# Local attention: two heads at once in the score products, native float32 in the value products

## Chip, cores and metric

The kernel runs on one core of a Trainium2 chip. The metric is the device time of one execution in microseconds; the kernel before takes 2477.17 us (median of 3 runs, 2470.8 to 2479.98).

## What is computed

A trunk of two layers on 512 tokens of width 1024. In each layer three mixers read the same normalised input `h`: (A) latent attention, (B) a gated recurrence in both directions, (C) attention in a window of 128 tokens to either side. Their outputs go through a projection each, are weighted by a gate and added; cross attention and a feed-forward block follow. The change lies in mixer C:

```python
q = q.reshape(Bsz, nb, C_BLOCK, C_KV_HEADS, G, C_DH)      # 8 heads of 64, 2 key heads, blocks of 128
s = einsum('bnqkgd,bnskd->bnkgqs', q, kb) * C_DH ** -0.5 + bias      # span of 3 blocks of keys
s = where(valid, s, MASK_VALUE)
m = maximum(max(s, axis=-1), sink_l)
p = exp(s - m)
p = p / (sum(p, axis=-1) + exp(sink_l - m))
o = einsum('bnkgqs,bnskd->bnqkgd', p, vb)
```

Everything is float32, and the result is compared with a float32 reference.

## The kernel before

Activations lie with the model dimension on the 128 partitions and the 512 tokens along the row. A product in near-float32 precision is made of three products in the one-pass type `fp32r`: every operand is split into a rounded part and a remainder (`split`, L177: a copy on ScalarE and a subtraction on VectorE), and `mm3` (L153) adds high·high, high·low and low·high in PSUM. Weights come from HBM as a stream of units of four 128x128 blocks in the order in which they are used (`_fetch`, L110, on SyncE's DMA queue; `_part`, L116, splits them); five buffers of raw and of split units let the stream run ahead. A projection of 1024 rows into 128 columns (`projs`, L164) is 24 matmuls of 512 columns and takes two units.

PSUM has eight banks, all of one pool (`bank`, L105). SBUF holds 25 buffers of 2 KB a partition (`t2`) and 14 of 8 KB (`c8`). A planner puts the instructions on each engine's queue: it goes by the order in the program as long as an instruction's inputs and its buffer are there, takes a later one where they are not, and places the semaphore waits. Every engine then works its queue strictly in that order.

Mixer C is `window_pre` (L698: keys, values and the first query, each a projection) and `window` (L726). One 128-row tile of the query holds two heads of 64 rows: head `bq` in rows 0 to 63 and head `bq + 4` in rows 64 to 127; the key tile has the two key heads in the same way. `window` goes through the eight heads one after the other, `i = 2 * bq + e`:

- `scores(bq, e)`, L742: fetches the head's bias block by DMA (L746), multiplies for each of four query blocks 64 rows of the query with 64 rows of keys (three products, 256 keys wide for the first and last block, 384 for the others), adds the bias out of PSUM into SBUF (L756), takes the row maximum (L757), and makes the normalised weights: maximum with the sink (L759), exponentials on ScalarE with their sums (L760, L762), sum, reciprocal, four multiplications (L764 to L767).
- the turn, L781 to L789: ten 128x128 transposes by TensorE, four banks, each split into a high and a low part.
- `values()`, L795: for four key blocks three products of the value block (128 columns, both key heads) with the turned weights. Only the 64 output rows of the head's own key head are kept (L802).

The scores of head `i + 1` are made behind the turn of head `i` and ahead of its values. Between a head's scores and its turn stand *fillers*: projections of mixer A's branch (`branch`, L507), put into a list and taken from it by `fill` (L186): two gates for an even head, for an odd head one `out` (two projections of four row blocks each, as long as one gate) and the projection of the next query (L780), whose split (`query`, L735) comes behind the turn. Mixer A (`mla`, L590) has the same stages; its values (`values`, L659) are native float32 products of 64 columns, two heads in the two column halves of the array.

Of the kernel before, what the change touches and what calls it, by code (L numbers as in the profile page):

```python
# [10 lines left out]
F32R = mybir.dt.float32r  # L11
I32 = mybir.dt.int32
AF = mybir.ActivationFunctionType
ALU = mybir.AluOpType
AX = mybir.AxisListType

P = 128
D = 1024
T = 512
# [19 lines left out]
V_GMIX, V_GX, V_GMEM, V_GFFN, V_GQ, V_GKV, V_GOUT, V_SINK, V_N = 0, 8, 16, 24, 32, 35, 37, 38, 46  # L39
# [36 lines left out]
class _K:  # L76
# [621 lines left out]
    def window_pre(self, l, h):  # L698

        st = self.wst_ = {}  # L700

        def step(nm, cols):
            def run():
                b, = self.projs("w_in", l, np.arange(D), [cols], h)
                if nm == "k":
                    kv = st["kv"] = self.c8([P, 4, T], F32R)
                    self.split(kv[:, 0], kv[:, 1], b)
                elif nm == "q":
                    st["q"] = (self.t2(F32R), self.t2(F32R))
                    self.split(st["q"][0], st["q"][1], b, scale=0.125)  # L710
                else:
                    kv = st["kv"]
                    vf = self.t2()
                    self.nc.scalar.activation(vf, b, AF.Copy)
                    tb = self.bank([P, 4, P])
                    for j in range(4):
                        self.nc.tensor.transpose(tb[:, j], vf[:, j * P:(j + 1) * P], self.ident)
                    st["v"] = [kv[:, 2 + i].rearrange("p (a b) -> p a b", a=4) for i in range(2)]
                    self.split(st["v"][0], st["v"][1], tb)
            return run  # L720
        return [step("k", O_KC + np.arange(P)), step("v", O_VC + np.arange(P)), step("q", self.qcol(0))]

# [3 lines left out]
    def window(self, l, h, y, before):  # L726
        nc = self.nc
        lv = V_N * l
        allr = np.arange(D)
        kv = self.wst_["kv"]  # L730
        k = (kv[:, 0], kv[:, 1])
        qt = self.wst_["q"]
        vh, vl = self.wst_["v"]

        def query(b):  # L735
            qt = (self.t2(F32R), self.t2(F32R))
            self.split(qt[0], qt[1], b, scale=0.125)
            return qt

        spans = [(P if j == 0 else 0, 256 if j == 3 else 384) for j in range(4)]  # L740

        def scores(bq, e):  # L742
            hd = bq + 4 * e
            a = slice(64 * e, 64 * e + 64)
            bias = self.t2(shape=(P, 384))
            nc.sync.dma_start(bias, self.biasd[hd])  # L746
            s = [self.t2(shape=(P, 384)) for _ in range(4)]
            st = self.sm(16, "smw", 4)
            nm, sm, es, rs = st[:, 0:4], st[:, 4:8], st[:, 8:12], st[:, 12:16]
            for j, (lo, hi) in enumerate(spans):  # L750
                sb = self.bank()
                js = slice(j * P, (j + 1) * P)
                ks = slice((j - 1) * P + lo, (j - 1) * P + hi)
                o = sb[:, :hi - lo]
                self.mm3(o, (qt[0][a, js], qt[1][a, js]), (k[0][a, ks], k[1][a, ks]), True, True)
                nc.vector.tensor_tensor(s[j][:, lo:hi], o, bias[:, lo:hi], op=ALU.add)  # L756
                nc.vector.reduce_max(nm[:, j:j + 1], s[j][:, lo:hi], axis=AX.X)  # L757
            sink = self.col(lv + V_SINK + hd)
            nc.vector.tensor_scalar(nm, nm, sink, -1.0, op0=ALU.max, op1=ALU.mult)  # L759
            nc.scalar.activation(es, nm, AF.Exp, bias=sink)  # L760
            for j, (lo, hi) in enumerate(spans):
                nc.scalar.activation(s[j][:, lo:hi], s[j][:, lo:hi], AF.Exp, bias=nm[:, j:j + 1],  # L762
                                     accum_out=sm[:, j:j + 1])
            nc.vector.tensor_tensor(es, es, sm, op=ALU.add)  # L764
            nc.vector.reciprocal(rs, es)
            for j, (lo, hi) in enumerate(spans):
                nc.vector.tensor_scalar(s[j][:, lo:hi], s[j][:, lo:hi], rs[:, j:j + 1], None, op0=ALU.mult)  # L767
            return s

        s = scores(0, 0)  # L770
        before()
        for i in range(8):
            bq, e = i // 2, i % 2
            a = slice(64 * e, 64 * e + 64)
            if i % 2 == 0:
                self.fill(2)
            else:
                self.fill(1 if bq < 3 else 2)
                if bq < 3:
                    qb = self.projs("w_in", l, allr, [self.qcol(bq + 1)], h)[0]  # L780
            pta, ptb = self.c8([P, 4, 384], F32R), self.c8([P, 4, 384], F32R)  # L781
            for kb in range(4):
                qs = [j for j in (kb - 1, kb, kb + 1) if 0 <= j < 4]
                tb = self.bank()
                for n, j in enumerate(qs):
                    c = (kb - j + 1) * P
                    nc.tensor.transpose(tb[:, n * P:(n + 1) * P], s[j][:, c:c + P], self.ident)  # L787
                w = len(qs) * P
                self.split(pta[:, kb, :w], ptb[:, kb, :w], tb[:, :w])  # L789
            if i < 7:  # L790
                if e == 1:
                    qt = query(qb)
                s = scores((i + 1) // 2, (i + 1) % 2)

            def values():  # L795
                o = self.bank()
                for kb in (0, 3, 1, 2):
                    q0 = max(kb - 1, 0) * P
                    w = 256 if kb in (0, 3) else 384
                    x = (pta[:, kb, :w], ptb[:, kb, :w])  # L800
                    self.mm3(o[:, q0:q0 + w], (vh[:, kb], vl[:, kb]), x, kb == 0, kb == 2)
                self.split(y[bq][0][a], y[bq][1][a], o[a])  # L802
            if i < 7:
                values()
        return values

    def memstat(self):

# [337 lines left out]
```

## Time and profile before

| | |
|---|---|
| median of 3 runs | 2477.17 us (2470.8 to 2479.98) |
| profiled execution | 2471.43 us, of which the span from first to last instruction is 2469.6 us |
| TensorE matmul busy | 2422.0 us, 98% |
| TensorE weight loads | 1999.7 us, 81% |
| VectorE / ScalarE / GpSimd busy | 1545.8 / 1215.4 / 262.6 us |
| granted clock of TensorE, mean | 0.995 |

Matmuls are pipelined, so that the busy times of neighbours overlap; the time from one start to the next says more than the length of one. Helpers hide the place of an instruction: nearly all products are of line 151, and they are told apart by the tiles and shapes. `128*64` is a product of 128 rows and 64 columns of the array; `64*128` one of 64 rows.

### The profile page before, as it was taken

What the parts mean: (1) busy time and instruction counts of PE and PEld (TensorE: products, weight loads), DVE (VectorE), ACT (ScalarE), POOL (GpSimd) and SP (SyncE); (2) the same over time, 40 slices, a digit from 0 to 9 for tenths busy, and PEclk for the clock granted to TensorE, in tenths of its full rate; (3) what the DMA queues carried; (4) which work ended last, traced back from release to release, by engine and by line L of the source; (5) the groups of instructions that cost most, each with busy time, mean ns of one, the idle gap of its engine ahead of it and who ended that gap; (6) DMA issues with size and microseconds to landing.
All of it is one profiled execution on the core that took longest, in us unless ns stands there. A gap on an engine that the chain in (4) does not pass through costs nothing.

```text
span 2469.6 us, 32711 instructions
## 1 busy us (share of the span) xinstructions
PE 2422.0 (98%) x12038; PEld 1999.7 (81%) x12038; DVE 1545.8 (63%) x2787; ACT 1215.4 (49%) x2213; POOL 262.6 (11%) x197
## 2 busy tenths in 40 slices
PE   8999999999999999999998999999999999999998
PEld 6788877788888888888877887887888888888886
DVE  8888666676665655355577776766766656553553
ACT  7666565455554533233466665654554445332332
POOL 2455300000000000000035542000000000000000
PEclk9999999999999999999999999999999999999999
DMA  4211322223453333333421222221224523333332
GB/s 140 70 61 55 90 74 60 63 73 100 140 138 98 86 95 98 96 96 98 129 73 60 69 74 63 73 64 60 81 79 149 146 78 89 97 96 98 98 96 76
DMA packets 119681, 220.96 MB, mean 89 GB/s; under 512 B 13281, under 2 KB 15585, under 8 KB 119137
## 3 DMA queue, kind: packets, MB, share of 16 engines
q1 hardware_dynamic: 119520, 218.88, 30.1%
q8 instruction: 94, 1.54, 0.3%
q14 instruction: 67, 0.54, 0.1%
HBM read 214.63 MB, written 4.19 MB: 89 GB/s over the span
## 4 chain that ended last, share of the span: by engine, by line
PE 82%; DVE 8%; issue 4%; ACT 3%; POOL 2%; DMA 1%; SPq 0%; DVEq 0%; ACTq 0%; POOLq 0%
PE ps L151 80%; POOL t L404 2%; DVE c L457 1%; PE ps L643 1%; DVE smx L411 1%; ACT whi L120 1%; POOL t L408 1%; DVE c L439 1%; DVE t L411 1%; DVE wlo L121 1%; PE ps L787 0%; DVE c L438 0%; DVE zz L482 0%; DMA c<-in_memT_dram 0%; DVE t L434 0%
## 5 line engine op out<-in xcount | busy, mean ns | idle before, releaser
L151 PE MATMUL ps<-c,whi 128*128 128x512 f32 (+1 forms) x5696 | 1734.7, 386 | 6.2 <-ACT whi L120 6.0
L151 PEld LDWEIGHTS ps<-c,whi 128*128 128x128 f32 x5696 | 1061.0, 188 | 227.7 <-issue 10.8
L151 PE MATMUL ps<-c,wlo 128*128 128x512 f32 (+1 forms) x2848 | 1098.9, 386 | 15.3 <-DVE wlo L121 15.2
L120 ACT ACTIVATE whi<-wraw 128x512 fp32r<-128x512 f32 x764 | 475.2, 630 | 841.7 <-PE ps L151 621.6
L121 DVE TENSOR_TENSOR wlo<-wraw,whi 128x512 fp32r<-128x512 f32 x764 | 520.2, 690 | 533.9 <-ACT whi L120 516.6
L151 PEld LDWEIGHTS ps<-c,wlo 128*128 128x128 f32 x2848 | 536.4, 188 | 126.7 <-DVE wlo L121 20.2
L151 PE MATMUL ps<-c,t 128*128 128x512 f32 (+4 forms) x896 | 185.6, 386 | 4.3 <-DVE c L181 2.8
L404 POOL TENSOR_SCALAR t<-t 128x512 f32<-128x512 f32 x32 | 71.7, 2242 | 1081.2 <-ACT t L401 1079.7
L151 PEld LDWEIGHTS ps<-c,t 128*128 128x128 f32 (+2 forms) x896 | 133.9, 182 | 43.6 <-issue 16.9
L457 POOL TENSOR_TENSOR c<-c,smx 128x256 f32<-128x256 f32 x128 | 145.0, 1161 | 74.3 <-DVE c L438 64.3
L966 DVE TENSOR_TENSOR t<-ps,t 128x512 f32<-128x512 f32 x112 | 76.2, 688 | 103.1 <-PE ps L151 103.1
L180 ACT ACTIVATE c<-ps 128x512 fp32r<-128x512 f32 (+3 forms) x200 | 97.7, 527 | 84.1 <-PE ps L151 81.3
L181 DVE TENSOR_TENSOR c<-ps,c 128x512 fp32r<-128x512 f32 (+3 forms) x200 | 114.9, 598 | 28.5 <-ACT c L180 27.4
L151 PE MATMUL ps<-c 128*32 128x32 f32 (+3 forms) x1280 | 108.1, 255 | 5.5 <-DVE c L439 5.5
L151 PEld LDWEIGHTS ps<-c 128*32 128x32 f32 (+2 forms) x1280 | 94.9, 148 | 21.3 <-DVE c L439 4.0
L948 DVE TENSOR_TENSOR c<-ps,c 128x512 f32<-128x512 f32 x64 | 44.2, 690 | 73.0 <-PE ps L151 73.0
L457 DVE TENSOR_TENSOR c<-c,smx 128x256 f32<-128x256 f32 x128 | 67.7, 587 | 0.3
L181 DVE TENSOR_TENSOR c<-t,c 128x512 fp32r<-128x512 f32 (+1 forms) x84 | 51.9, 633 | 2.9 <-ACT c L180 2.9
L408 POOL TENSOR_TENSOR t<-t,t 128x512 f32<-128x512 f32 x32 | 44.7, 1397 | 84.1 <-ACT t L407 84.1
L180 ACT ACTIVATE c<-t 128x512 fp32r<-128x512 f32 (+1 forms) x84 | 47.8, 581 | 9.4 <-DVE t L390 3.3
L406 ACT ACTIVATE t<-t 128x512 f32<-128x512 f32 x32 | 20.1, 629 | 62.4 <-POOL t L404 62.4
L411 DVE TENSOR_TENSOR_SCAN t<-cst,t 128x512 f32<-128x512 f32 x32 | 40.8, 1275 | 15.8 <-POOL t L408 15.8
(144 smaller groups left out, 1888.7 us busy)
## 6 DMA issues: line engine op xcount, KB each, us to landing
wraw<-in_w_dram SPq DMA_DIRECT2D x764, 256.0 KB, 2.7
c<-in_xT_dram SPq DMA_DIRECT2D x16, 256.0 KB, 5.1
t<-in_bias_dram SPq DMA_DIRECT2D x16, 192.0 KB, 2.8
c<-in_memT_dram SPq DMA_DIRECT2D x3, 1024.0 KB, 8.0
xs<-c SPq DMA_DIRECT2D x8, 256.0 KB, 2.4
c<-xs SPq DMA_DIRECT2D x8, 256.0 KB, 4.3
out_dram<-t SPq DMA_DIRECT2D x8, 256.0 KB, 2.0
t<-in_rope_dram SPq DMA_DIRECT2D x4, 256.0 KB, 3.1
```

The costliest lines, as they stand in the source:

```text
L120: self.nc.scalar.activation(hi, raw, AF.Copy)
L121: self.nc.vector.tensor_tensor(lo, raw, hi.bitcast(F32), op=ALU.subtract)
L151: self.nc.tensor.matmul(o, a, b, start=start, stop=stop)
L180: nc.scalar.activation(hi, src, AF.Copy)
L181: nc.vector.tensor_tensor(lo, src, hi.bitcast(F32), op=ALU.subtract)
L404: nc.gpsimd.tensor_scalar(g, f, TINY, KNEE, op0=ALU.max, op1=ALU.min)
L408: nc.gpsimd.tensor_tensor(f, f, g, op=ALU.add)
L411: scan = lambda o, m, x: nc.vector.tensor_tensor_scan(o, m, x, 0.0, op0=ALU.mult, op1=ALU.add)
L439: nc.vector.scalar_tensor_tensor(ki, kk, omlb, cc, op0=ALU.mult, op1=ALU.mult)
L457: eng.tensor_tensor(ov, sv, ev, op=ALU.mult)
L948: nc.vector.tensor_tensor(x[c], b, xold[c], op=ALU.add)
L966: self.nc.vector.tensor_tensor(t, b, r, op=ALU.mult)
```

## The change

The scores of two heads are made together, their products alternating between the array's row halves, in two banks for each block; adding the bias and taking the maximum is one instruction, which starts from the sink. The turned weights are copied once in float32 instead of being split, and the values are one native float32 product a head and block, 64 columns wide, both heads into one bank. The query's projection comes ahead of the odd head's filler.

```diff
-        def scores(bq, e):
-            hd = bq + 4 * e
...
+        def scores(bq):
+            hds = [bq, bq + 4]
+            biases, ss, sts, os = [], [], [], []
+            for e in range(2):
+                bias = self.t2(shape=(P, 384))
+                nc.sync.dma_start(bias, self.biasd[hds[e]])
...
             for j, (lo, hi) in enumerate(spans):
-                self.mm3(o, (qt[0][a, js], qt[1][a, js]), (k[0][a, ks], k[1][a, ks]), True, True)
-                nc.vector.tensor_tensor(s[j][:, lo:hi], o, bias[:, lo:hi], op=ALU.add)
-                nc.vector.reduce_max(nm[:, j:j + 1], s[j][:, lo:hi], axis=AX.X)
+                os.append([self.bank()[:, :hi - lo] for _ in range(2)])
+                for n, (qi, ki) in enumerate(((0, 0), (0, 1), (1, 0))):
+                    for e in range(2):
+                        a = slice(64 * e, 64 * e + 64)
+                        self.mm(os[j][e], qt[qi][a, js], k[ki][a, ks], n == 0, n == 2)
+                for e in range(2):
+                    nc.vector.tensor_tensor_reduce(ss[e][j][:, lo:hi], os[j][e], biases[e][:, lo:hi], 1.0,
+                                                   self.col(lv + V_SINK + hds[e]), ALU.add, ALU.max,
+                                                   sts[e][0][:, j:j + 1])
...
+        def turned(s):
+            pt = self.c8([P, 4, 384])
...
-                self.split(pta[:, kb, :w], ptb[:, kb, :w], tb[:, :w])
+                if kb % 2 == 0:
+                    nc.scalar.activation(pt[:, kb, :w], tb[:, :w], AF.Copy)
+                else:
+                    nc.vector.tensor_copy(pt[:, kb, :w], tb[:, :w])
...
-                    self.mm3(o[:, q0:q0 + w], (vh[:, kb], vl[:, kb]), x, kb == 0, kb == 2)
-                self.split(y[bq][0][a], y[bq][1][a], o[a])
+                    for e in range(2):
+                        a = slice(64 * e, 64 * e + 64)
+                        self.mm(o[a, q0:q0 + w], v[:, kb, a], pts[e][:, kb, :w], kb == 0, kb == 2)
+                self.split(y[bq][0], y[bq][1], o)
...
+        ss = scores(0)
+        before()
+        for bq in range(4):
+            self.fill(2)
+            pts = [turned(ss[0])]
+            if bq < 3:
+                qb = self.projs("w_in", l, allr, [self.qcol(bq + 1)], h)[0]
+                self.fill()
+            else:
+                self.fill(2)
+            pts.append(turned(ss[1]))
+            pend = values(bq, pts)
+            if bq < 3:
+                qt = query(qb)
+                ss = scores(bq + 1)
+                pend()
+        return pend
```

## Rows read from the trace of the kernel before

**Rows 1.** The page: span, and busy time, share and instructions of each engine.
```profile
span 2469.6 us, 32711 instructions
PE 2422.0 (98%) x12038; PEld 1999.7 (81%) x12038; DVE 1545.8 (63%) x2787; ACT 1215.4 (49%) x2213; POOL 262.6 (11%) x197
```
**Rows 2.** The page: the chain that ended last, shares of the span by engine.
```profile
PE 82%; DVE 8%; issue 4%; ACT 3%; POOL 2%; DMA 1%; SPq 0%; DVEq 0%; ACTq 0%; POOLq 0%
```
**Rows 3.** Windows of the stage in either layer: busy time (count) by engine, clock, DMA.
```profile
476.46:613.70 137.24, 136.63 (x698) 115.02 (x697) 93.87 (x217) 74.66 (x172) 0.00 (x0) 1.00 0.28 84
1765.20:1842.00 76.80, 76.39 (x395) 65.42 (x394) 50.80 (x116) 41.68 (x94) 0.00 (x0) 1.00 0.27 83
```
**Rows 4.** TensorE in order of time, odd head: start, us, what, count.
```profile
493.03 1.25 PE L787 MATMUL ps<-cst,t 128*128 128x128 f32 x10
494.21 2.04 PE L151 MATMUL ps<-c,t 64*128 64x256 f32 x12
496.18 2.02 PE L151 MATMUL ps<-c,c 128*128 128x256 f32 x12
498.05 0.63 PE L151 MATMUL ps<-c,whi 128*128 128x512 f32 x2
```
**Rows 5.** TensorE in order of time, the even head after it.
```profile
508.97 1.25 PE L787 MATMUL ps<-cst,t 128*128 128x128 f32 x10
510.43 2.02 PE L151 MATMUL ps<-c,t 64*128 64x256 f32 x12 [0.21 <-ACT t L183]
512.38 0.74 PE L151 MATMUL ps<-c,c 128*128 128x256 f32 x4
```
**Rows 6.** Groups by shape, whole span: half of the score matmuls.
```profile
L151 PE MATMUL ps<-c,t 64*128 64x256 f32 x96 | 19.0, 294 | 1.2 <-ACT t L183 1.2
```
**Rows 7.** Mixer A's values in column halves: weight loads in order of time, and what follows.
```profile
478.43 0.20 PEld L151 LDWEIGHTS ps<-c,t 128*64 128x64 f32 x4
478.91 0.14 PEld L151 LDWEIGHTS ps<-c,t 128*64 128x64 f32 x2 [0.29 <-issue]
...
481.06 0.14 PEld L151 LDWEIGHTS ps<-c,t 128*64 128x64 f32 x2 [0.28 <-issue]
...
482.02 0.73 PE L151 MATMUL ps<-c,whi 128*128 128x512 f32 x2
```
**Rows 8.** TensorE in order of time: a turn that ends in a projection.
```profile
605.38 1.25 PE L787 MATMUL ps<-cst,t 128*128 128x128 f32 x10
606.39 0.71 PE L151 MATMUL ps<-c,whi 128*128 128x512 f32 x2
```
**Rows 9.** Groups by shape, whole span: adding the bias and the maximum on VectorE.
```profile
L756 DVE TENSOR_TENSOR t<-ps,t 128x384 f32<-128x384 f32 x32 | 17.5, 546 | 0.0
L757 DVE TENSOR_REDUCE smw<-t 128x1 f32<-128x384 f32 x32 | 17.3, 541 | 0.0
L756 DVE TENSOR_TENSOR t<-ps,t 128x256 f32<-128x256 f32 x32 | 13.3, 415 | 10.1 <-DMA t<-in_bias_dram 10.1
```
**Rows 10.** VectorE in order of time behind the scores of the even head.
```profile
510.60 0.68 DVE L184 SCALAR_TENSOR_TENSOR t<-ps,t 128x512 fp32r<-128x512 f32 x1
...
515.27 0.89 DVE L756 TENSOR_TENSOR t<-ps,t 128x256 f32<-128x256 f32 x2 [2.73 <-DMA t<-in_bias_dram]
...
517.66 0.87 DVE L757 TENSOR_REDUCE smw<-t 128x1 f32<-128x384 f32 x2
...
522.47 1.28 DVE L767 TENSOR_SCALAR t<-t,smw 128x256 f32<-128x256 f32 x4
```
**Rows 11.** SyncE's queue in order of time: bias DMAs of an odd and an even head.
```profile
492.09 0.42 SPq L746 DMA_DIRECT2D t<-in_bias_dram  x1
...
508.20 2.50 SPq L112 DMA_DIRECT2D wraw<-in_w_dram  x2
510.75 0.42 SPq L746 DMA_DIRECT2D t<-in_bias_dram  x1
```
**Rows 12.** Line 746, the bias DMA: from issue to landing.
```profile
DMA to landing us min/median/max: 2.7/2.8/4.4
```

More of the change, by code (lines that the diff above doesn't have):

```diff
@@ L705, in run @@
                 if nm == "k":
-                    kv = st["kv"] = self.c8([P, 4, T], F32R)
+                    kv = st["kv"] = self.c8([P, 2, T], F32R)
                     self.split(kv[:, 0], kv[:, 1], b)
@@ L711, in run @@
                 else:
-                    kv = st["kv"]
                     vf = self.t2()
@@ L717, in run @@
                         self.nc.tensor.transpose(tb[:, j], vf[:, j * P:(j + 1) * P], self.ident)
-                    st["v"] = [kv[:, 2 + i].rearrange("p (a b) -> p a b", a=4) for i in range(2)]
-                    self.split(st["v"][0], st["v"][1], tb)
+                    st["v"] = self.t2(shape=(P, 4, P))
+                    self.nc.scalar.activation(st["v"], tb, AF.Copy)
             return run
@@ L732, in window @@
         qt = self.wst_["q"]
-        vh, vl = self.wst_["v"]
+        v = self.wst_["v"]
         def query(b):
@@ L740, in window @@
         spans = [(P if j == 0 else 0, 256 if j == 3 else 384) for j in range(4)]
-        def scores(bq, e):
-            hd = bq + 4 * e
[L744 to L749, printed above, removed]
+        def scores(bq):
[4 more added lines that the diff above has]
+                nc.sync.dma_start(bias, self.biasd[hds[e]])
+                biases.append(bias)
+                ss.append([self.t2(shape=(P, 384)) for _ in range(4)])
+                st = self.sm(16, "smw", 4)
+                sts.append([st[:, i:i + 4] for i in range(0, 16, 4)])
@@ L750, in scores @@
             for j, (lo, hi) in enumerate(spans):
-                sb = self.bank()
                 js = slice(j * P, (j + 1) * P)
                 ks = slice((j - 1) * P + lo, (j - 1) * P + hi)
-                o = sb[:, :hi - lo]
-                self.mm3(o, (qt[0][a, js], qt[1][a, js]), (k[0][a, ks], k[1][a, ks]), True, True)
-                nc.vector.tensor_tensor(s[j][:, lo:hi], o, bias[:, lo:hi], op=ALU.add)
-                nc.vector.reduce_max(nm[:, j:j + 1], s[j][:, lo:hi], axis=AX.X)
@@ L758, in scores @@
[L758 to L781, printed above, removed]
+                os.append([self.bank()[:, :hi - lo] for _ in range(2)])
@@ new lines, in scores @@
+            for e in range(2):
+                s, (nm, sm, es, rs) = ss[e], sts[e]
+                nc.vector.tensor_scalar(nm, nm, -1.0, None, op0=ALU.mult)
+                nc.scalar.activation(es, nm, AF.Exp, bias=self.col(lv + V_SINK + hds[e]))
+                for j, (lo, hi) in enumerate(spans):
+                    nc.scalar.activation(s[j][:, lo:hi], s[j][:, lo:hi], AF.Exp, bias=nm[:, j:j + 1],
+                                         accum_out=sm[:, j:j + 1])
+                nc.vector.tensor_tensor(es, es, sm, op=ALU.add)
+                nc.vector.reciprocal(rs, es)
+                for j, (lo, hi) in enumerate(spans):
+                    nc.vector.tensor_scalar(s[j][:, lo:hi], s[j][:, lo:hi], rs[:, j:j + 1], None, op0=ALU.mult)
@@ L782, in window @@
+            return ss
+        def turned(s):
+            pt = self.c8([P, 4, 384])
             for kb in range(4):
@@ L788, in window, with values, run @@
                 w = len(qs) * P
-                self.split(pta[:, kb, :w], ptb[:, kb, :w], tb[:, :w])
[L790 to L795, printed above, removed]
+                if kb % 2 == 0:
+                    nc.scalar.activation(pt[:, kb, :w], tb[:, :w], AF.Copy)
+                else:
+                    nc.vector.tensor_copy(pt[:, kb, :w], tb[:, :w])
+            return pt
+        def values(bq, pts):
+            def run():
                 o = self.bank()
@@ L799, in values @@
                     w = 256 if kb in (0, 3) else 384
-                    x = (pta[:, kb, :w], ptb[:, kb, :w])
-                    self.mm3(o[:, q0:q0 + w], (vh[:, kb], vl[:, kb]), x, kb == 0, kb == 2)
-                self.split(y[bq][0][a], y[bq][1][a], o[a])
-            if i < 7:
-                values()
-        return values
+                    for e in range(2):
+                        a = slice(64 * e, 64 * e + 64)
+                        self.mm(o[a, q0:q0 + w], v[:, kb, a], pts[e][:, kb, :w], kb == 0, kb == 2)
+                self.split(y[bq][0], y[bq][1], o)
+            return run
+        ss = scores(0)
[15 more added lines that the diff above has]
+        return pend
     def memstat(self):
```

## The prediction

> **What bounds the kernel now.** I read the page's engine shares first [rows 1]: TensorE is busy for 2422.0 of 2469.6 us, VectorE for 63%, ScalarE for 49%. The chain of waits puts 82% of the span on TensorE [rows 2], so what the array does not have to do is worth its full length wherever nothing else becomes late. Then the two stretches in which the change lies, by windows [rows 3]: local attention of layer 0 (476.46 to 613.70) keeps the array busy for 136.63 of 137.24 us at the full granted clock (1.00), VectorE for 93.87, ScalarE for 74.66. Layer 1 looks the same. So the stage is bound by TensorE with 0.6 us idle, and the two engines that empty PSUM have a third to a half of their time free.
>
> Busy time of pipelined matmuls overlaps, so I price by the time from the start of one group to the start of the next. A head is ten transposes, twelve score matmuls, twelve value matmuls, then two fillers or a filler and a query projection. For an odd head [rows 4]: transposes 494.21 − 493.03 = 1.18 us, scores 496.18 − 494.21 = 1.97, values 498.05 − 496.18 = 1.87, and 48 projection matmuls up to 508.97, 10.92. The next, even head [rows 5] has 1.46 us from transposes to scores, because the scores stood 0.21 us for the split of a fresh query on ScalarE; its scores take 512.38 − 510.43 = 1.95. There are 16 heads in all; of their 192 score matmuls 96 are 256 wide [rows 6], the others 384.
>
> **The change, part by part.**
>
> *Scores.* The count stays 24 for a pair of heads, but the two heads alternate, one in array rows 0 to 63 and one in 64 to 127, in banks of their own. If the halves run side by side, a pair takes what one head takes now, 1.95 us instead of 3.90: 8 pairs × 1.95 = 15.6 us gained. The trace has no row halves side by side. The far end is that they queue: gain 0, the 1.95 us a head of [rows 5]. The nearest row for the other end is the previous stage's values, where two heads share the array by column halves [rows 7]: the weight loads come in pairs, a pair every (481.06 − 478.91)/5 = 0.43 us, so two independent halves do run at once. Between the two are weight loads that queue though the products overlap: ten transposes of 128 columns pass in 1.18 us with a load each, so 24 loads at 0.11 us are 2.6 us a pair instead of 1.95, 5 us less gain in all. I take the full 15.6, the row nearest in kind.
>
> *Values.* Before, three fp32r products into 128 columns for each of four key blocks and each head: 1.87 × 2 = 3.74 us a pair. After, native float32 with 64 columns a head, which is the form of [rows 7]: a 512-wide product is two records of 0.43 us, two heads at once. Per pair of heads: key blocks 256, 256, 384, 384 wide are 2 × 0.43 × (256 + 256 + 384 + 384)/512 = 2.15 us. The edges are (482.02 − 478.43) − 8 × 0.43 = 0.15 us, and 0.11 more because the first two projection matmuls after it take 0.73 us together rather than 0.62. Sum 2.41; gain 1.33 × 8 = 10.6 us. Both forms stand in the trace, so this term is the surest. Would the halves queue, a pair would be 4.6 us, a loss; the paired loads exclude it.
>
> *Transposes.* Twenty a pair, as before. But one of the two groups now ends in a projection instead of in scores, 606.39 − 605.38 = 1.01 us plus 0.09 for the next two matmuls [rows 8], against 1.18; and the query's projection is moved ahead of a filler, so that its split is long done when the scores come and the 1.46 falls to 1.18. Three pairs a layer go from 2.64 to 2.28 and the last from 2.28 to 2.20: 1.2 us a layer, 2.3 in all; 0.6 if the wait for the query stays.
>
> *VectorE and ScalarE.* For every block an add and a maximum (0.546 + 0.541 us at 384 wide, the add 0.415 at 256 [rows 9]) become one add-and-reduce. Nothing like it is in the trace; it lies between the add alone and add plus maximum, so a pair's eight take 3.84 to 7.6 us where sixteen took 7.6. The splits of the turned weights become plain copies, half of them on each engine, and the values' split is one for two heads. All that is work off an engine that waits anyway; I price it at nothing. What it hides behind is the stretch from a pair's scores to the first transposes of its weights: 1.95 + 2.41 + 10.92 = 15.3 us. The even head of [rows 10] needs 523.75 − 515.27 = 8.5 us from its first add to its last normalised row, 3.3 of it adds and maxima; with eight reductions for both heads in that place it is 9.1 to 12.8. That is in time, also if it starts 2 us into the scores.
>
> *PSUM and the bias.* This is the wait that the change adds. A pair's scores take all eight banks. The values that stand right behind them on TensorE, and with them every filler, need a bank, so they wait for the first add-and-reduce, and that waits for a bias block by DMA. Today four banks stay free, and a late bias shows only on VectorE: in [rows 10] the adds began at 515.27, 4.84 us after their scores at 510.43, having stood idle for 2.73 for the DMA, and TensorE went on. The DMA left SyncE only at 510.75, behind a weight fetch and 0.15 us after VectorE took up the query's split at 510.60 [rows 10, 11]; landing takes 2.7 to 4.4 us [rows 12]. Behind an odd head it leaves about 2 us ahead of the scores, at 492.09 [rows 11]. After the change the pair's two bias DMAs still stand behind the query, but the query's projection now ends a filler and a group of transposes, 5.5 + 1.2 us, ahead of the scores. If the planner lets them follow the split, they land in time: the first reduction starts about 0.6 us into the scores, when the first block's quarter of the 1.95 us is through, and with 0.42 to 0.82 us for it a bank is free at 1.0 to 1.4, before the 1.95. So I cost it at nothing; the other end is the first rival. If the second head's bias is the later one, that harms nothing: four banks are free by then.
>
> SyncE gets the same 16 bias DMAs; two now stand together, 0.42 us each, in front of the next weight fetch, which has five buffers and runs units of 2.7 us ahead (twelve matmuls at 10.92/48 us). The other edits (the value block kept as one float32 tile, a smaller key tile) change a copy and a split a layer, off the path.
>
> Sum: 15.6 + 10.6 + 2.3 = 28.5 us. The profiled execution took 2471.43 us, 5.7 below the median of the runs (2477.17). Off the profiled one that leaves 2443; off the median, which I forecast, 2448.7, so **2449 us**.
>
> **Rivals.**
>
> *1. The banks come late.* The biases leave when they leave for an even head now, 0.3 us after the scores begin, land at 3.0 to 4.7, and with one reduction (0.42 to 0.82) the first bank is free at 3.4 to 5.5 instead of 1.95: 1.5 to 3.5 us stand on TensorE for the three pairs of a layer that come behind a query's projection (the first pair's query is made before the stage). Six times that is 9 to 21, so 2458 to 2470, middle 2464. For it: adds waited 10.1 us for a bias in all [rows 9], the even head's 2.73 among them. Against: the query comes earlier. The Trainium skill points this way: "TensorEngine Tiling (Array Packing)", Performance Considerations, says that tiling speeds up the array but not the emptying of PSUM, which can become the bound, and its Gotcha 1 that row tiles want banks of their own. The trace so far shows neither, for it has no row tiles in pairs.
>
> *2. The row halves do not overlap*, the change not doing what it says: 28.5 − 15.6 = 12.9 gained, 2464. For it: no row shows it. Against: the column halves overlap, in loads and products.
>
> *3. Every switch between the row halves drains the array.* It is the one way I see to slower. The place is the 24 alternating score matmuls; the price is in the trace, for going from full-height transposes to half-height scores costs nearly 0.2 us (1.18 against 1.01 us [rows 4, 8]). With 0.1 us at each of 23 switches in 8 pairs, 18 us are lost and no overlap is left: 12.9 − 18.4 = −5.5, about 2483. From 0.07 a switch it decides the sign. Against it: column halves alternate without a pause, four loads in 0.20 us [rows 7]. The same page, Key Properties, has a change of mode drain the array and a change of tile not; by that this rival falls, and the first term stands.
>
> **How the numbers follow.** Forecast 0.62 (its own range 2440 to 2457: the queued loads, a stray microsecond per pair, the spread of the runs); late banks 0.18; no overlap 0.12; drains or another mishap 0.08. The range 2440 to 2468 holds the first three but for the worst of the late banks. About 0.5%, 12.4 us, is what can be told from no change here: below 2464.8 the kernel is faster. The forecast is all on that side, late banks a little over half of the time, no overlap half: 0.62 + 0.10 + 0.06 = 0.78. Slower 0.07; the rest, 0.15, is same.
>
> **What would show it.** In the profile after: score matmuls of two heads starting within some 10 ns, and some 1.95 us from the first to the values (3.9: rival 2; over 4.5: rival 3). Values a pair 2.4 us. No idle time of TensorE put down to the new reduction; some 2 us of it ahead of the values, six times, is rival 1, and the bias DMA's issue against the first score says why. The reduction's mean at 384 wide between 0.55 and 1.09 us. I am wrong in kind if the stage's two windows shrink by less than 20 us with all of these in place: then the time went to the weight stream or to the order of the fillers.

## The result, and the profile after

The changed kernel takes 2446.15 us (median of four runs, 2444.95 to 2447.82) against 2478.27 us for the kernel before (median of four, 2470.80 to 2479.98). The ratio over all runs is 0.9877, with a 95% interval of 0.9855 to 0.9898; the two medians alone give 0.9870. The forecast was 2449, within 2440 to 2468, so it is faster, by 32.1 us between the medians. Its profiled execution took 2445.72 us, 25.7 less than the one of before [rows 1]. That the two differences disagree by 6.4 us is explained at the end of this section.

The page of the kernel after: the span, the engines' shares, and the chain by engine.
```profile
span 2443.9 us, 32499 instructions
PE 2396.9 (98%) x11974; PEld 1966.2 (80%) x11974; DVE 1503.9 (62%) x2745; ACT 1194.2 (49%) x2169; POOL 262.9 (11%) x197
...
PE 85%; DVE 8%; ACT 3%; POOL 2%; issue 1%; DMA 1%; SPq 0%; DVEq 0%; ACTq 0%; POOLq 0%
```
TensorE was busy for 25.1 us less than in [rows 1], out of a span that is 25.7 shorter, and its share of the chain rose from 82% [rows 2] to 85%; no other engine's share of the chain grew. So nearly all of the gain is work that the array no longer has. VectorE also lost 41.9 us; whether that mattered is a question for the experiments.

The stage in layer 0 of the kernel after, and then in layer 1: windows from the first score to the end of the last values, with busy time (count) of PE, PEld, DVE, ACT, POOL, the granted clock, DMA share, GB/s.
```profile
478.99:602.15 123.16, 123.16 (x665) 97.53 (x664) 73.55 (x198) 64.60 (x152) 0.00 (x0) 1.00 0.30 92
1690.22:1813.35 123.13, 123.13 (x665) 97.53 (x665) 73.01 (x196) 63.32 (x147) 0.00 (x0) 1.00 0.28 83
```
Against 137.24 us [rows 3] layer 0 is 14.08 shorter. The second window of [rows 3] is only a part of layer 1's stage (76.80 us), so it can't be compared; the whole of layer 1 before is one more window of that kernel:
```profile
1701.79:1838.99 137.20, 136.59 (x697) 114.98 (x697) 93.94 (x216) 74.00 (x169) 0.00 (x0) 1.00 0.26 76
```
So layer 1 gave 14.07, and the stage gave 28.15 us in all, for 28.5 in the prediction's sum. TensorE is busy for every microsecond of it; the 0.6 us that stood idle in [rows 3] are gone.

One pair of heads in TensorE's order of time after (start, us, what, count), seen twice: first only what runs in the 0.12 us up to 508.82, then the whole way from the transposes to the projection.
```profile
508.80 0.39 PE L151 MATMUL ps<-c,t 64*128 64x256 f32 x2
```
```profile
507.62 1.25 PE L784 MATMUL ps<-cst,t 128*128 128x128 f32 x10
508.80 4.32 PE L151 MATMUL ps<-c,t 64*128 64x256 f32 x40
513.06 0.74 PE L151 MATMUL ps<-c,whi 128*128 128x512 f32 x2
```
Within 20 ns of 508.80 two score products have begun (3 ns apart by the trace); in the kernel before, the second one of [rows 5] began 0.22 us after the first. The row of 40 holds 24 score and 16 value products, since the view joins neighbours; the weight loads part them, because the scores load 128 columns and the values 64:
```profile
508.80 1.82 PEld L151 LDWEIGHTS ps<-c,t 64*128 64x128 f32 x24 [0.17 <-issue]
...
510.75 1.06 PEld L151 LDWEIGHTS ps<-c,t 128*64 128x64 f32 x12
...
513.05 0.30 PEld L151 LDWEIGHTS ps<-c,whi 128*128 128x128 f32 x2 [0.60 <-DVE smw L761]
```
From the scores to the values it is 510.75 − 508.80 = 1.95 us for two heads, which one head took before [rows 5], and the values end at 513.06, 2.31 later. The 24 loads passed in 1.82 us. Before, the twelve of one head took as long:
```profile
494.21 1.83 PEld L151 LDWEIGHTS ps<-c,t 64*128 64x128 f32 x12 [0.17 <-issue]
```
The 0.60 us that the loads stood for the reduction is no loss: it is the bank of the projection, and the products were still at the values.

VectorE in order of time behind a later pair (scores from 537.32), and SyncE's bias DMAs for that pair:
```profile
538.34 0.47 DVE L761 CUSTOM_DVE_ANT_0 t<-ps,t,small 128x256 f32<-128x256 f32 x1
...
547.61 1.28 DVE L774 TENSOR_SCALAR t<-t,smw 128x256 f32<-128x256 f32 x4
```
```profile
529.38 0.33 SPq L112 DMA_DIRECT2D wraw<-in_w_dram  x1
529.76 0.90 SPq L747 DMA_DIRECT2D t<-in_bias_dram  x2
```
The biases left 7.6 us ahead of the scores, right behind a weight fetch, and were there (a bias DMA lands 2.6 to 3.6 us after its issue). The first reduction began 1.02 us into the scores and ended 0.4 to 0.5 later, before the 1.95 were up. The last normalised rows of both heads were done at 548.89, before the first of the pair's two turns began at 552.63.

The groups by shape over the whole span after, the new reduction:
```profile
L761 DVE CUSTOM_DVE_ANT_0 t<-ps,t,small 128x384 f32<-128x384 f32 x32 | 17.8, 611 | 0.0
L761 DVE CUSTOM_DVE_ANT_0 t<-ps,t,small 128x256 f32<-128x256 f32 x32 | 14.1, 477 | 0.0
L761 DVE DVE_READ_ACCUMULATOR2_ANT smw<- 128x1 f32 x64 | 5.2, 81 | 0.0
```
The idle column is 0.0: VectorE never stood for a bias, where it had stood 10.1 us in [rows 9].

Where the other microseconds of the two differences are: outside of the stage the program is the same, but its first matmuls met different clocks. Windows of the first small products in mixer B, of the kernel after and then of the kernel before:
```profile
50.00:57.00 7.00, 3.84 (x17) 2.70 (x15) 6.40 (x15) 5.22 (x10) 5.21 (x5) 0.99 0.20 51
57.00:67.00 10.00, 9.34 (x72) 7.94 (x73) 9.15 (x15) 4.69 (x9) 4.39 (x5) 0.50 0.39 123
```
```profile
50.00:57.00 7.00, 3.84 (x17) 2.72 (x15) 6.40 (x15) 5.21 (x10) 5.21 (x5) 1.00 0.19 43
57.00:67.00 10.00, 9.33 (x85) 8.22 (x86) 9.96 (x17) 6.85 (x14) 4.40 (x5) 0.83 0.43 129
```
Product by product the two executions run within 0.02 us of each other from 17 to 59 us, and stay 2.5 to 2.6 us apart from 69 us up to the stage. In both, TensorE had been idle for almost half of the first 7 us shown; then one had the lower level (1.2 GHz) throughout the 10 us, the other for part of it. The stage after began 478.99 − 476.46 = 2.53 us later with it, and 28.15 − 2.53 = 25.6 is the difference of the two spans but for 0.1. The median of before lies 6.8 us above its profiled time, that of after 0.4 above: the rest is which execution was profiled.

### The profile page after: what moved, and what is told of

It reads as the page before. It is cut to its first block, busy times and chain, and to the rows that moved or that the text cites. A ratio compares the mean times of both kernels' runs of the same rounds, so it can differ in the third digit from the quotient of the medians.

```text
span 2443.9 us, 32499 instructions
## 1 busy us (share of the span) xinstructions
PE 2396.9 (98%) x11974; PEld 1966.2 (80%) x11974; DVE 1503.9 (62%) x2745; ACT 1194.2 (49%) x2169; POOL 262.9 (11%) x197
## 4 chain that ended last, share of the span: by engine, by line
PE 85%; DVE 8%; ACT 3%; POOL 2%; issue 1%; DMA 1%; SPq 0%; DVEq 0%; ACTq 0%; POOLq 0%
PE ps L151 83%; POOL t L404 2%; DVE c L457 1%; PE ps L643 1%; DVE smx L411 1%; PE ps L784 1%; POOL t L408 1%; DVE c L439 1%; DVE t L411 1%; DVE wlo L121 1%; DVE c L181 0%; ACT whi L120 0%; DVE c L438 0%; DVE zz L482 0%; DMA c<-in_memT_dram 0%
## 5 line engine op out<-in xcount | busy, mean ns | idle before, releaser
L151 PEld LDWEIGHTS ps<-c,whi 128*128 128x128 f32 x5696 | 1059.4, 188 | 232.8 <-issue 10.4
L151 PE MATMUL ps<-c,wlo 128*128 128x512 f32 (+1 forms) x2848 | 1098.4, 386 | 15.3 <-DVE wlo L121 15.2
L121 DVE TENSOR_TENSOR wlo<-wraw,whi 128x512 fp32r<-128x512 f32 x764 | 521.0, 690 | 552.9 <-ACT whi L120 539.8
L151 PE MATMUL ps<-c,t 128*128 128x512 f32 (+6 forms) x1024 | 188.0, 393 | 4.0 <-DVE c L181 3.7
L151 PEld LDWEIGHTS ps<-c,t 128*128 128x128 f32 (+2 forms) x1024 | 127.8, 176 | 48.0 <-issue 20.2
L181 DVE TENSOR_TENSOR c<-ps,c 128x512 fp32r<-128x512 f32 (+2 forms) x126 | 80.2, 650 | 23.7 <-ACT c L180 23.4
L180 ACT ACTIVATE c<-ps 128x512 fp32r<-128x512 f32 (+2 forms) x126 | 68.4, 565 | 43.9 <-PE ps L151 42.6
```

What stands on the lines that cost most here:

```text
L121: self.nc.vector.tensor_tensor(lo, raw, hi.bitcast(F32), op=ALU.subtract)
L151: self.nc.tensor.matmul(o, a, b, start=start, stop=stop)
L180: nc.scalar.activation(hi, src, AF.Copy)
L181: nc.vector.tensor_tensor(lo, src, hi.bitcast(F32), op=ALU.subtract)
```

## Experiments

Because of the spread just shown the kernels are compared by the stage's window in layer 0 (123.16 us after), and by the ratio to the kernel before where three rounds were run.

**1. Do the halves overlap because two heads alternate?** All twelve products of one head, then all of the other:

```
-for j, (lo, hi) in enumerate(spans):
     ...
-    for n, (qi, ki) in enumerate(((0, 0), (0, 1), (1, 0))):
-        for e in range(2):
+for e in range(2):
+    for j, (lo, hi) in enumerate(spans):
         ...
+        for n, (qi, ki) in enumerate(((0, 0), (0, 1), (1, 0))):
             self.mm(os[j][e], qt[qi][a, js], k[ki][a, ks], n == 0, n == 2)
```

> Changed kernel, but all twelve score products of the first head (array rows 0 to 63) come before the twelve of the second (rows 64 to 127); everything else as changed. Theory (the gain of the scores is that two row halves run at once when they alternate): only the last product of the one head can overlap the first of the other, so the scores of a pair go from 1.95 to 3.7 to 3.8 us, 1.8 x 8 pairs = 14 to 15 us on the whole kernel, and the stage of layer 0 from 123.2 to about 130.4 us. Rival (the halves do not overlap, the gain comes from elsewhere, such as fewer switches between full and half height): scores stay at 1.95 us and the time at that of the changed kernel.

Measured: 2458.87 us, ratio 0.9931 (0.9916 to 0.9945), against 0.9877 for the change. TensorE at one pair: what runs up to 510.90, then the scores of the whole pair, and the first weight loads of the values; below it the stage's window.
```profile
510.88 0.38 PE L151 MATMUL ps<-c,t 64*128 64x256 f32 x1
...
510.88 3.35 PE L151 MATMUL ps<-c,t 64*128 64x256 f32 x24
...
514.16 1.06 PEld L151 LDWEIGHTS ps<-c,t 128*64 128x64 f32 x12
```
```profile
479.71:608.23 128.52, 128.52 (x665) 102.88 (x664) 73.92 (x198) 64.90 (x152) 0.00 (x0) 1.00 0.29 88
```
One product begins where two had, and a pair's scores take 3.28 us up to the values (510.88 to 514.16) instead of 1.95. The stage is 5.36 us longer a layer, four times 1.34. So the side-by-side halves are what the scores gained: the same products with the same operands cost 1.34 us more a pair when they are not offered beside each other. It was less than the 3.7 to 3.8 expected, because the heads overlapped where they meet: the second head's first product began 7 ns after the first head's ninth, ahead of that head's last three, and the three products of the 256-wide block on either side ran beside each other (so in all eight pairs).

**2. Does it hang on the query's projection standing a filler ahead?** Filler and projection exchanged:

```
 if bq < 3:
-    qb = self.projs("w_in", l, allr, [self.qcol(bq + 1)], h)[0]
     self.fill()
+    qb = self.projs("w_in", l, allr, [self.qcol(bq + 1)], h)[0]
```

> Changed kernel with the filler ahead of the query's projection again, as before the change. Theory of the prediction: the scores wait some 0.27 us for the query's split, three times a layer (1.6 us in all); and the two bias DMAs, which had come 7.6 us ahead of the scores in the changed kernel, come with the query's split, about 0.3 us after the scores begin, land at 3 to 4.7 us, and hold the eight banks: 1.5 to 3.5 us of TensorE idle ahead of the values, six times, 9 to 21 us together. Rival (the early bias has another reason, such as the buffers that the change frees): biases stay several us ahead of the scores, TensorE loses only the 1.6 us.

Measured: 2459.8 us (one run), the stage 6.08 us longer. The stage, and TensorE, SyncE and VectorE at the second pair:
```profile
476.83:606.07 129.24, 124.89 (x666) 97.91 (x665) 74.45 (x198) 64.82 (x152) 0.00 (x0) 1.00 0.28 88
```
```profile
506.84 1.20 PE L151 MATMUL ps<-c,t 64*128 64x256 f32 x11
508.20 1.26 PE L151 MATMUL ps<-c,t 64*128 64x256 f32 x13 [0.17 <-DVE t L184]
510.58 2.37 PE L151 MATMUL ps<-c,t 128*64 128x256 f32 x16 [1.12 <-DVE smw L761]
```
```profile
501.50 5.61 SPq L112 DMA_DIRECT2D wraw<-in_w_dram  x3
507.16 0.90 SPq L747 DMA_DIRECT2D t<-in_bias_dram  x2
```
```profile
510.03 0.48 DVE L761 CUSTOM_DVE_ANT_0 t<-ps,t,small 128x256 f32<-128x256 f32 x1 [1.88 <-DMA t<-in_bias_dram]
```
This is the prediction's first rival: the biases leave 0.32 us after the scores began, the first reduction waits for them until 510.03, and the values, which need its bank, start at 510.58, 3.74 us behind the scores instead of 1.95. It happens in three of four pairs a layer, as was said; part of it is the split of the query (0.17 us here, and a start 0.23 us later). The biases left right behind a weight fetch here, too: the last of the three above went at 506.78, 0.03 us after VectorE had split an earlier unit (L121), and the bias 0.05 us behind it.

**3. What was the native float32 worth?** The values go back to three fp32r products a key block and head, with the splits in place of the copies; the key tile moves to two smaller buffers to make room:

```
-pt = self.c8([P, 4, 384])
+pt = (self.c8([P, 4, 384], F32R), self.c8([P, 4, 384], F32R))
 ...
+self.split(pt[0][:, kb, :w], pt[1][:, kb, :w], tb[:, :w])
 ...
-self.mm(o[a, q0:q0 + w], v[:, kb, a], pts[e][:, kb, :w], kb == 0, kb == 2)
+self.mm3(o[:, q0:q0 + w], (v[0][:, kb], v[1][:, kb]), x, kb == 0, kb == 2)
```

> Changed kernel with the values as before the change: turned weights and value block split in a high and a low part, three products of 128 columns for each head and block (the key tile moved to two small buffers to make room). Theory: values of a pair 3.75 us instead of 2.30 + 0.11, so 1.34 x 8 = 10.7 us lost; the doubled work of ScalarE and VectorE in the turn costs nothing. Rival (the split was on the path, and the copies in its place a part of the gain): more than 14 us lost, with TensorE waiting for the split ahead of the values. Other rival (values bring nothing): under 3 us lost.

Measured: 2464.83 us, ratio 0.9957 (0.9941 to 0.9974); the stage 8.04 us longer where 5.3 was expected. The stage, and TensorE, its weight loads and VectorE at the second pair:
```profile
479.19:610.39 131.20, 130.68 (x698) 108.31 (x697) 83.95 (x219) 73.08 (x174) 0.00 (x0) 1.00 0.31 88
```
```profile
508.98 3.17 PE L151 MATMUL ps<-t,t 64*128 64x256 f32 x24
512.08 3.78 PE L151 MATMUL ps<-c,t 128*128 128x256 f32 x24
515.70 0.63 PE L151 MATMUL ps<-c,whi 128*128 128x512 f32 x2
```
```profile
510.28 0.18 PEld L151 LDWEIGHTS ps<-t,t 64*128 64x128 f32 x1 [0.47 <-DVE c L181]
510.74 1.21 PEld L151 LDWEIGHTS ps<-t,t 64*128 64x128 f32 x11 [0.28 <-DVE c L181]
```
```profile
509.81 1.68 DVE L181 TENSOR_TENSOR c<-ps,c 128x256 fp32r<-128x256 f32 x4
511.40 0.48 DVE L761 CUSTOM_DVE_ANT_0 t<-ps,t,small 128x256 f32<-128x256 f32 x1
```
The values take 515.70 − 512.08 = 3.62 us instead of 2.31: that is the prediction's term. The rest was not expected. The scores now take 512.08 − 508.98 = 3.10, since four splits of the turned weights on VectorE hold their banks until 511.5, and the later scores, which want all eight, wait for them. So with the row halves in place the copies are not free: three pairs a layer pay 1.15 us for the splits, 6.9 in all. The loss, 18.7 us between the medians, has the size that the rival named (more than 14), but the wait lies inside the scores and not ahead of the values.

**4. Was the add-and-reduce worth anything?** An add and a maximum again, with the sink's maximum taken once for four blocks:

```
-nc.vector.tensor_tensor_reduce(ss[e][j][:, lo:hi], os[j][e], biases[e][:, lo:hi], ...)
+nc.vector.tensor_tensor(ss[e][j][:, lo:hi], os[j][e], biases[e][:, lo:hi], op=ALU.add)
+nc.vector.reduce_max(sts[e][0][:, j:j + 1], ss[e][j][:, lo:hi], axis=AX.X)
 ...
-nc.vector.tensor_scalar(nm, nm, -1.0, None, op0=ALU.mult)
+nc.vector.tensor_scalar(nm, nm, self.col(lv + V_SINK + hds[e]), -1.0, op0=ALU.max, op1=ALU.mult)
```

> Changed kernel with the add-and-reduce taken apart again into an add and a maximum (16 instructions a pair instead of 8). Theory: VectorE has that time, so the stage stays at 123.2 us within 0.5 us and TensorE waits for nothing new. Rival (the eight banks make VectorE the bound at the scores): the banks come free a maximum later each, 0.41 to 0.54 us, and fillers or values wait: 0.5 us or more a pair, 4 us or more in all.

Measured: 2447.93 us (one run). Its stage:
```profile
478.28:601.45 123.17, 123.17 (x665) 97.57 (x664) 84.01 (x198) 65.17 (x152) 0.00 (x0) 1.00 0.31 92
```
VectorE has 10.5 us more to do and the stage is as long as after. So the single instruction in place of two gained nothing here.

**5. Must the heads alternate product by product?** In each block three products of the first head, then three of the second:

```
-for n, (qi, ki) in enumerate(((0, 0), (0, 1), (1, 0))):
-    for e in range(2):
+for e in range(2):
+    for n, (qi, ki) in enumerate(((0, 0), (0, 1), (1, 0))):
```

> Changed kernel, but in each block the first head's three score products come before the second head's three (with all twelve before all twelve a pair's scores had taken 3.28 us instead of 1.95, and only where the heads met did two products start together). Theory (TensorE starts products in order, and one may start beside its predecessor only if that lies in the other row half): of six products in a block the first of a head starts beside the last of the other, so four slots instead of three with alternation or six without; scores of a pair 4/3 of 1.75 plus 0.2 = 2.5 us, 0.6 lost a pair, 4.7 us in all. Rival (any order overlaps as long as both halves have work in the queue): 1.95 us, nothing lost.

Measured: 2441.68 us (one run). TensorE up to 506.71, and the scores of the pair; below it the stage:
```profile
506.69 0.39 PE L151 MATMUL ps<-c,t 64*128 64x256 f32 x2
...
506.69 2.02 PE L151 MATMUL ps<-c,t 64*128 64x256 f32 x24
```
```profile
476.70:600.06 123.36, 123.36 (x666) 97.74 (x665) 73.55 (x198) 64.57 (x152) 0.00 (x0) 1.00 0.31 92
```
My theory, that products start in the order of the queue so that three and three cannot overlap from the start, fell. Two began within 20 ns (10 by the trace) though the second stood fourth by the program, and the pair took 1.955 us. The description of the kernel before has every engine work its queue strictly in order; the starts of TensorE's products do not keep to that here, nor where the heads meet in experiment 1. Only the first pair of each layer took longer, 2.13. The 4.5 us by which this run is below the median of after are not the stage's, which is 0.20 longer; in the stretch from 53 to 72 us it had a granted clock of 0.91 where the profiled execution after had 0.73, which is 2.3 of them, since its stage began at 476.70; the rest was not traced.

**6. How much of experiment 2 was the bias?** The query late, as there, but the bias tiles in two buffers of their own instead of the shared pool (which has 23 for it, not 25):

```
-NT2 = 25
+NT2 = 23
 ...
-bias = self.t2(shape=(P, 384))
+bias = self.tl("bias", [P, 384], F32, 2)
 ...
```

> The run with the query's projection behind the filler, which lost 12 us in the two stages (scores to values 3.74 us instead of 1.95), with the two bias blocks in buffers of their own, two of them taken from the 25, so that their DMA can leave as soon as the pair before is done with them. Theory (what cost 1.8 us a pair was the bias that lands late and with it the banks): bias DMAs many us ahead of the scores, scores to values 2.0 to 2.2 us, 9 to 11 of the 12 us come back; what stays is the wait for the query's split, some 0.3 to 0.4 us, three times a layer. Rival (it is the late query itself that holds up the scores): scores to values stay over 3 us.

Measured: 2452.64 us (one run). The stage; a pair's scores; their weight loads; the pair's bias DMAs:
```profile
482.92:608.53 125.61, 124.63 (x666) 97.90 (x665) 73.96 (x198) 64.64 (x152) 0.00 (x0) 1.00 0.32 93
```
```profile
512.93 1.20 PE L151 MATMUL ps<-c,t 64*128 64x256 f32 x11 [0.16 <-ACT t L183]
514.29 3.57 PE L151 MATMUL ps<-c,t 64*128 64x256 f32 x29 [0.17 <-DVE t L184]
```
```profile
512.92 0.88 PEld L151 LDWEIGHTS ps<-c,t 64*128 64x128 f32 x11 [0.40 <-ACT t L183]
514.29 2.25 PEld L151 LDWEIGHTS ps<-c,t 64*128 64x128 f32 x25 [0.49 <-DVE t L184]
```
```profile
487.63 0.99 SPq L747 DMA_DIRECT2D bias<-in_bias_dram  x2
```
The biases now leave 25 us ahead of the scores, and no value waits for a reduction. Of the 6.08 us of experiment 2, 129.24 − 125.61 = 3.63 were the bias, 1.2 for each of three pairs. The other 2.45 are the split of the late query, 0.8 a pair, by the waits for lines 183 and 184: the scores begin 0.23 us later and take 2.56 us instead of 1.95. That is twice the 0.3 to 0.4 expected, and less came back than was expected (7.3 us over both layers, not 9 to 11). The smaller pool has a price of its own ahead of the stage: it began at 482.92, where experiment 4, with the same granted clock from 53 to 72 us (0.82), had 478.28.

**7. Does the form carry to mixer B?** Its values, too, in native float32 column halves, two heads in one pass, with copies for splits:

```
 ...
+for e, ae in enumerate((even, a)):
+    hf = slice(64 * e, 64 * e + 64)
+    self.mm(ob[hf], vs[pr][:, j, hf], ae[:, s], j == 0, j == 3)
-self.mm3(ob, (vh[:, j], vl[:, j]), (a[0][:, s], a[1][:, s]), j == 0, j == 3)
 ...
```

> Changed kernel, and the values of mixer B (the gated recurrence) in the same form: the decayed scores of a head kept once in float32 instead of split, the value block too, and both heads' products of 64 columns in the column halves, native float32, made behind the second head. Theory from the term of the values: 24 products of 512 columns, 24 x 0.227 = 5.45 us a pair, become 16 records, 8 x 0.43 + 0.26 = 3.70 us: 1.75 us a pair, 8 pairs, 14 us; with some of the waits for the split that this stage shows (2.4 us at one head of layer 0) gone as well. About 2430 us. Rival (mixer B is bound by VectorE, ScalarE and GpSimd around the decay, and the array's time is spare there): under 5 us gained, with TensorE waiting for the decay or its copies instead.

Measured: 2422.24 us (2420.36 to 2427.22), ratio 0.9782 (0.9755 to 0.981): faster than both kernels, some 24 us below the changed one. The values of one pair here; and, in the kernel after, the odd head of the first pair and the even one of the second.
```profile
108.22 3.65 PE L151 MATMUL ps<-c,t 128*64 128x512 f32 x16
111.80 0.73 PE L151 MATMUL ps<-c,whi 128*128 128x512 f32 x2
```
```profile
114.30 0.63 PE L151 MATMUL ps<-c,t 128*128 128x512 f32 x1
116.70 2.79 PE L151 MATMUL ps<-c,t 128*128 128x512 f32 x11 [1.77 <-DVE c L181]
...
149.96 2.89 PE L151 MATMUL ps<-c,t 128*128 128x512 f32 x12
```
A pair takes 3.58 us where an even head took 2.72 and an odd one 3.03 to 5.03, with the wait for its split; over the eight heads of layer 0 that is 14.3 for 25.2 us. Local attention begins at 465.80 instead of 478.99, 13.2 earlier, and 25.4 earlier in layer 1. It was more than the 14 us expected because waits for splits went, too: those at the odd heads, which are part of the 25.2 us, and some for the splits of weights (L121), for which the array waited 3.6 us between 100 and 345 us, where it had waited 5.8.

## Why the prediction was right

That the total came within 3 us of 2449 is partly luck, since the four runs of the kernel before spread over 9.2 us. The stage is the better test: 28.15 us for 28.5, and term by term as follows.

*What bounds the stage.* Right: a product less is its full length less, down to TensorE busy for 123.16 of 123.16 us. Experiment 4 shows the other side, VectorE's work at no price.

*Scores, 15.6.* Measured 15.6: the scores of layer 0 took 15.61 us before and 7.81 after, by the starts of the groups, so 7.80 a layer. The full overlap was the right end. The bound between, loads that queue at 0.11 us each, did not come: the 24 loads of a pair passed in 1.82 us, no longer than the twelve of one head before (1.83). Experiment 1 confirms the cause.

*Values, 10.6.* Measured 10.4: 14.91 before and 9.22 after in layer 0, 5.69 gained, less about half (an estimate: the increase stands behind values and behind transposes alike) of the 0.94 us by which the projections grew (93.02 to 93.96), which the prediction had put at 0.11 behind values and 0.09 behind transposes. The pair takes 2.31 + 0.13 for 2.41.

*Transposes, 2.3.* 10.12 before and 8.59 after in layer 0, 1.53, less the other half of that 0.94: 1.06 a layer, 2.1 in all. What stood against this term was put too low: left late, the query costs 2.45 us a layer even with the biases early (experiment 6), where the prediction took off 1.7 us for both layers together.

*VectorE and ScalarE at nothing.* Right for the reduction, which at 0.61 us (384 wide) plus 0.08 to read it out lies within the 0.55 to 1.09. The reason given was too narrow for the copies: the prediction looked at the 15.3 us from scores to transposes, and not at the banks that the turn's splits hold when the next scores want all eight. Experiment 3 puts 6.9 us on that. It was no loss of the change, since copies came with it, but the gain of the scores alone, with the old values, would have been smaller by it: experiment 3 is that kernel, and 0.9957 leaves it 10.6 us, where the terms for scores and transposes add up to 17.9. So the terms do not simply add.

*PSUM and the bias.* Right in the outcome, and experiment 2 shows the wait in the place and with the reason given: three pairs a layer, a bias DMA 0.32 us behind the first score, the values behind the reduction. The values stood 3.74 − 1.95 = 1.8 us longer behind the scores, near the low end of the range of 1.5 to 3.5; the bias alone is 1.2 of it (experiment 6). One step was off in its reason. The biases do not leave with the split of the query: at 529.76 they left 1.45 us before VectorE or ScalarE took up that query's split (531.21). What held them at run time was their place in SyncE's queue: in the kernel after and in experiment 2 alike they left 0.05 us behind a weight fetch, and that had waited for VectorE to split an earlier unit (L121). Experiment 6 shows what set the place: with buffers of their own, and the pool two smaller, but otherwise as in experiment 2, they leave 25 us early. So the turn of the shared pool put them there, and the exchange of filler and projection moved it; that the biases came in time was right by luck in this step. The first reduction began at 1.02 and not 0.6 us, behind a copy of VectorE's, and still in time.

The Trainium skill's sentence on this, in "TensorEngine Tiling (Array Packing)", Performance Considerations, that tiling does not speed up the emptying of PSUM, which may then bind, is borne out in experiments 2 and 3 only in part, and in another form than a lack of throughput: VectorE is idle for 42% and 36% of these two stages, and what binds is how long a single bank is held (1.12 us of wait for the reduction, 0.47 + 0.28 for the splits).

*Rivals 2 and 3.* Both fell. The halves overlap, and there is no drain: 24 alternating products leave 1.95 us, 23 switches of 0.07 to 0.1 would have added 1.6 to 2.3. The Trainium skill, on the same page, Key Properties, has only a change of mode drain the array; as to the change of tile the trace agrees, by this 1.95 us.

## What to carry to other kernels

Products of half the array's height took half the time here when two independent ones were offered beside each other or a few places apart, in row halves and banks of their own; then look at who holds the banks, since a stage that fills all eight can turn a late reduction, split or DMA into time of TensorE. A wait like that is often decided far from the edit, here by the place of a DMA in a queue behind a weight fetch, which moves with the turn of a buffer pool and the order of a filler and a projection. And where a form has paid in one stage, look for the old form in others: mixer B gave another 24 us.

## What the runs showed of the hardware that was not expected

- TensorE starts a product of the other row half ahead of its turn: with three and three in the program's order two began 10 ns apart (experiment 5), and with twelve and twelve the thirteenth began beside the ninth, three places early but not sooner (experiment 1). How far ahead it looks was not measured apart.
- Weight loads of the two row halves run beside each other, too: 24 of 64 rows passed in 1.82 us in turn between the halves, twelve of one half in 1.83.
- Executions of the same instructions differ by some microseconds in the first 70 us, with the granted clock: 0.73, 0.82 or 0.91 in the mean over 53 to 72 us, in eight profiled executions with the same products up to there, each value more than once. Window by window of the stage is the comparison that this does not touch.
